# Layer 0's attention: the order of some VectorE operations, and the engine of a few others

## The chip, the cores and the metric

The kernel runs on one core of a Trainium2 chip. A core has five engines, each with a queue of its own that it works through in order: TensorE (PE: matmuls; PEld is its weight load), VectorE (DVE), ScalarE (ACT), GpSimd (POOL) and SyncE (SP, which here only issues transfers). Semaphores hold an engine until what it needs is there. The metric is device time in microseconds.

## The reference, cut to what matters

Two layers of a transformer trunk over 512 latent and 256 context tokens, width 1024. In each layer a modulated norm and one input projection give attention operands (`q`, `k`, `v`) and the two inputs of a gated mixer (`u`, `vg`); both results go through one output projection, then a feed-forward part follows.

```python
def chunk_gmlp(u, vg, w_s, b_s, g_norm):
    b, n, _ = u.shape
    u = jax.nn.gelu(u)
    vg = group_layernorm(jax.nn.gelu(vg).reshape(b, n, N_GMLP_GROUPS, GMLP_GROUP_DIM),
                         g_norm.reshape(N_GMLP_GROUPS, GMLP_GROUP_DIM))
    vc = vg.reshape(b, n // CHUNK, CHUNK, N_GMLP_GROUPS, GMLP_GROUP_DIM)
    mixed = jnp.einsum('gpq,bnqgc->bnpgc', w_s, vc) + b_s.T[None, None, :, :, None]
    return u * mixed.reshape(b, n, GMLP_DIM)

for l in range(DEPTH):
    ...
    attn_lat = gqa_blocks(qh_l, k_all, v_all)
    gm_lat = chunk_gmlp(u_l, g_l, w_spatial[l], b_spatial[l], gmlp_norm_g[l])
    x_lat = x_lat + ga1 * (jnp.concatenate([attn_lat, gm_lat], axis=-1) @ w_out[l])
    x_lat = x_lat + ga2 * sqrelu_mlp(modulate(rmsnorm(x_lat, norm2_g[l]), sh2, sc2),
                                     w_ff1[l], w_ff2[l])
```

Layer 0 does the same for the context tokens, whose queries see only the context's 256 keys.

## The kernel before

**Products.** Large products are taken from two parts of each operand, a rounded high one and the remainder, in three matmuls (high by high, high by low, low by high). `split` makes the parts: ACT casts the high one (L221), DVE or POOL subtracts to get the low one (L222). Weights go through a ring: SP loads `raw`, and `split` fills `hi` and `lo`. The low parts of the output projection's weights are made on POOL.

**The gated mixer of layer 0.** The 768 tokens are taken as three pairs of 128-token chunks and two halves of the channels: six *mixing halves*, numbered n = 0 to 5. The fifth half is n = 4, the last n = 5. For each, `sink_g` takes the projected bank through a GELU (L817 to L822) to `s`. Then `rest` computes mean and variance of four groups (L874, L875), adds an epsilon (L877), takes the inverse root on POOL (L298, by `rsqrt`), normalises the four groups in place (L880, four instructions) and splits `s` into `e` (ACT) and a low part (`acc` on DVE for the last half, a second `e` on POOL otherwise). `mixing` multiplies with the spatial weights `ws` into a PSUM bank `pt` (L217), scales and adds the bias on DVE (L905, two instructions, which empty the bank) and multiplies with `u` on POOL (L910, into `C`). When all are done, `make_gm` splits the gated result into the operands `A0` to `A3` of the output projection: a cast on ACT (L783) and a subtraction (L784), on POOL for the first two and on DVE for the other two.

**Attention of layer 0.** The context block (four pairs of query heads, two heads, two tiles) comes first. `attn_tile` makes the scores in a bank `pa`, their maximum on DVE (L999), the exponential on ACT (L1002, `w`), its reciprocal on DVE (L1004) and a copy of it on POOL (L1007). Later pieces transpose `w` on PE (L1018) into a `pt` bank, and split it with a cast on ACT (L1020) and a subtraction on DVE (L1021), then multiply with V (`third`, L1042 to L1045).

**What fills the gaps.** While attention runs, PE also works on the second half of layer 0's modulation (L354, its sums turned by L362 and L367 and added by L437), and then on the output projection of the gated result, whose results DVE adds into the residual (L954). The constants of the next layer are loaded and scaled by `consts`: the pack `k2` is issued by ACT (L652), then L660 twice, L671 and L674 scale it on DVE.

**What sets the order.** One program text is traced in order, and the engine queues follow from it. A planner, `Flow`, has a virtual time that matmuls move ahead. `defer(delay, f)` sets a due time for a piece, and `tick` runs what is due. `PAR` holds these delays: `G0` is 13600 from the end of `rest` to `mixing`; for the last half of layer 0, `rest` itself is deferred by 8000 and `mixing` by 8000 + `G0`. A scheduler then orders the instructions of each engine within that. DVE, ACT and POOL run what stands in their queues strictly in order.

## Time and profile before

| | us |
|---|---|
| median of 3 runs | 1482.96 (1482.33 to 1485.31) |
| the profiled execution | 1483.62 |
| its span | 1481.5 |
| mean granted PE clock | 0.998 |
| ACT busy | 635.9 (43%) |
| POOL busy | 363.5 (25%) |

The profile is of one execution; its time stands beside its span, and what lies around the span is 2.1 us. A row of the timeline gives start, duration, engine, line, operation and operands, then in brackets how long the engine sat idle before it and what ended that. Line numbers are those of the kernel before. In the 35 us from 165 to 200 us all of the instructions stand that the change moves.

### The profile page before, as it was taken

Reading aid. Unit: us, or ns where it says so; the run is one execution under the profiler, and the core shown is the slowest. Engines: PE = TensorE matmul, PEld = TensorE weight load, DVE = VectorE, ACT = ScalarE, POOL = GpSimd, SP = SyncE. Lnnn points to the kernel's source line nnn. Section 1 sums busy time; section 2 is a strip of 40 time slices with the busy share of each in tenths; the row PEclk is TensorE's granted clock in tenths of the full one; section 3 lists DMA queues with packets and bytes.
Section 4 is the critical chain, followed back from the end, with each engine's and each line's share of the span. In section 5 each row is a group of like instructions: output and inputs, shape, how many; then the busy total and the mean of one; then the engine's idle time right before and its main releaser. Section 6 shows DMA issues by size and latency. Waiting matters only on the chain.

```text
span 1481.5 us, 21923 instructions
## 1 busy us (share of the span) xinstructions
PE 1446.6 (98%) x8626; PEld 1275.9 (86%) x8626; DVE 879.6 (59%) x1543; ACT 635.9 (43%) x1081; POOL 363.5 (25%) x347
## 2 busy tenths in 40 slices
PE   6999899999999999999999999999999999999998
PEld 2899677898899999999989989998899888888887
DVE  5857767787755554544454437867877554444443
ACT  3552446673545453334334224536865322332221
POOL 0323521322064461413132213166122000000000
PEclk9999999999999999999999999999999999999999
DMA  9322444101233333424333311222001333222221
GB/s 367 111 72 83 167 148 160 58 16 58 75 121 121 115 121 107 142 100 135 107 128 114 100 43 58 101 72 61 26 1 59 128 100 99 89 97 100 100 100 57
DMA packets 50087, 148.78 MB, mean 100 GB/s; under 512 B 5440, under 2 KB 6976, under 8 KB 49984
## 3 DMA queue, kind: packets, MB, share of 16 engines
q1 hardware_dynamic: 49408, 146.72, 29.4%
q8 instruction: 68, 1.11, 0.3%
q10 hardware_dynamic: 576, 0.66, 0.1%
q14 instruction: 35, 0.29, 0.1%
HBM read 145.26 MB, written 2.10 MB: 99 GB/s over the span
## 4 chain that ended last, share of the span: by engine, by line
PE 85%; DVE 7%; ACT 3%; POOL 2%; issue 2%; DMA 1%; SPq 0%; POOLq 0%; ACTq 0%; DVEq 0%
PE pa L217 55%; PE pb L217 22%; PE pt L1018 3%; PE pt L217 2%; PE pb L354 2%; POOL m L298 1%; DVE s L880 1%; POOL lo L222 1%; DVE lo L222 1%; DMA A<-in_w_mod 1%; PE pt L735 1%; ACT hi L221 0%; DVE bn L874 0%; DVE s L822 0%; ACT w L1002 0%
## 5 line engine op out<-in xcount | busy, mean ns | idle before, releaser
L217 PE MATMUL pa<-A,hi 128*128 128x384 f32 (+2 forms) x1664 | 441.1, 347 | 1.0 <-DVE s L706 0.8
L221 ACT CAST hi<-raw 128x1024 fp32r<-128x1024 f32 x168 | 176.4, 1051 | 449.3 <-PE pa L217 364.6
L222 DVE TENSOR_TENSOR lo<-raw,hi 128x1024 fp32r<-128x1024 f32 x152 | 193.7, 1275 | 230.9 <-ACT hi L221 227.3
L217 PEld LDWEIGHTS pa<-A,hi 128*128 128x128 f32 x1664 | 299.4, 188 | 21.9 <-DVE s L706 1.0
L217 PE MATMUL pa<-A,lo 128*128 128x384 f32 (+2 forms) x832 | 287.9, 346 | 0.0
L217 PE MATMUL pa<-B,hi 128*128 128x512 f32 (+1 forms) x900 | 241.0, 355 | 0.0
L403 POOL TENSOR_TENSOR C<-C,s 128x512 f32<-128x512 f32 x112 | 162.9, 1469 | 310.7 <-ACT s L402 309.4
L217 PEld LDWEIGHTS pa<-B,hi 128*128 128x128 f32 x900 | 159.7, 189 | 24.2
L217 PEld LDWEIGHTS pa<-A,lo 128*128 128x128 f32 x832 | 156.5, 188 | 10.1
L217 PE MATMUL pa<-B,lo 128*128 128x512 f32 (+1 forms) x450 | 159.5, 355 | 0.0
L217 PE MATMUL pb<-B,hi 128*128 128x512 f32 (+1 forms) x600 | 157.3, 350 | 2.0 <-DVE X L954 2.0
L954 DVE SCALAR_TENSOR_TENSOR X<-pa,modT,X 128x512 f32<-128x512 f32 x126 | 79.4, 658 | 128.7 <-PE pa L217 128.7
L954 DVE SCALAR_TENSOR_TENSOR X<-pb,modT,X 128x512 f32<-128x512 f32 (+3 forms) x116 | 70.9, 619 | 82.2 <-PE pb L217 82.0
L217 PE MATMUL pb<-hi,A 128*128 128x256 f32 (+1 forms) x608 | 118.1, 291 | 0.6 <-DVE m L715 0.6
L217 PEld LDWEIGHTS pb<-B,hi 128*128 128x128 f32 x600 | 103.6, 189 | 16.5 <-DVE X L954 3.0
L217 PE MATMUL pb<-B,lo 128*128 128x512 f32 (+1 forms) x300 | 104.1, 347 | 0.0
L217 PEld LDWEIGHTS pb<-hi,A 128*128 128x128 f32 x608 | 97.0, 191 | 2.2 <-PE pb L217 0.8
L402 ACT ACTIVATE s<-k,silu 128x512 f32<-128x512 f32 x112 | 77.1, 716 | 44.8 <-DMA k<-in_w_mod 31.0
L217 PEld LDWEIGHTS pa<-B,lo 128*128 128x128 f32 x450 | 84.9, 189 | 12.0
L217 PE MATMUL pb<-lo,A 128*128 128x256 f32 (+1 forms) x304 | 87.7, 288 | 0.0
L217 PE MATMUL pb<-A,hi 128*128 128x384 f32 (+2 forms) x288 | 80.9, 361 | 2.3 <-ACT A L783 0.9
L1021 DVE TENSOR_TENSOR A<-pt,A 128x384 fp32r<-128x384 f32 (+1 forms) x144 | 73.1, 535 | 9.9 <-ACT A L1020 8.2
(197 smaller groups left out, 2221.8 us busy)
## 6 DMA issues: line engine op xcount, KB each, us to landing
raw<-in_w_ff SPq DMA_DIRECT2D x128, 512.0 KB, 3.5
k<-in_w_mod SPq DMA_DIRECT2D x96, 256.0 KB, 3.0
raw<-in_w_tok SPq DMA_DIRECT2D x16, 512.0 KB, 3.5
raw<-in_w_out SPq DMA_DIRECT2D x16, 512.0 KB, 3.5
lo<-in_w_mod SPq DMA_DIRECT2D x16, 512.0 KB, 4.5
hi<-in_w_mod SPq DMA_DIRECT2D x16, 512.0 KB, 4.0
A<-in_w_mod SPq DMA_DIRECT2D x8, 512.0 KB, 10.1
B<-in_w_mod SPq DMA_DIRECT2D x8, 512.0 KB, 9.5
```

Of the source, the lines that this page charges most:

```text
L217: pe.matmul(out, a, b, start=start, stop=stop)
L221: act.copy(hi, src)
L222: (eng or vec).tensor_tensor(out=lo, in0=src, in1=hi.bitcast(F32), op=ALU.subtract)
L298: pool_e.tensor_tensor(out=y, in0=v, in1=mhalf[:, 0:n], op=ALU.pow)
L354: pe.matmul(ps[q:q + 32, :], S32[:, k, :], ws_[k2 // 2][:, k2 % 2 * 512:(k2 % 2 + 1) * 512], start=k < ns, stop=k >= KT - ns)
L402: act.activation(p, w, AF.Copy, scale=s)
L403: pool_e.tensor_tensor(out=a, in0=a, in1=p, op=ALU.add)
L735: pe.transpose(p[:, o:o + 128], stk[:, t, hh, c0:c0 + 128].bitcast(F32), ident)
L880: (pool_e if l in PAR['VG'] else vec).tensor_scalar(v[:, i * 128:i * 128 + 128], v[:, i * 128:i * 128 + 128], mv[:, i, 0:1], r[:, i:i + 1] ...
L954: vec.scalar_tensor_tensor(out=xs, in0=src[:, s - off:e - off], scalar=modT[l][:, i * 8 + m, cond:cond + 1], in1=xs, op0=ALU.mult, op1=ALU ...
L1018: pe.transpose(tp_[:, (kt - k0) * 128:(kt - k0) * 128 + 128], p[:, kt * 128:kt * 128 + 128], ident)
L1021: vec.tensor_tensor(out=ptl[:, k0:k0 + step, d], in0=src, in1=pth[:, k0:k0 + step, d].bitcast(F32), op=ALU.subtract)
```

## The change

It has four parts, all in layer 0's attention.

- The last two mixing halves. `rest` is cut in two: `first` (statistics and inverse root) and `rest` (normalisation and split). The normalisation of the fifth half is issued behind the first attention tile's maximum (`maxes[0]`), that of the last half behind the second L905 of the half before (`evicted`). Four due times in `PAR` (`E0` to `E3`) take the place of the 8000 and of the sum with `G0`.
- All four low parts of `make_gm` are made on DVE, in layer 0 behind the fourth tile's maximum (`maxes[3]`) where there is one.
- The last of the six gated products (L910) is made on DVE.
- The next layer's constants are scaled on ACT.

```diff
@@ -39,7 +39,7 @@
        "FG0": [[0, 1], [2, 3]], "FG1": [[0, 1], [2], [3]], "QK0": 10000.0, "QK1": 9300.0, "TURN0": 3600.0,
        "TURN1": 5800.0, "G0": 13600.0, "G1": 22100.0, "T0": 6600.0, "T1": 7000.0, "TC": 1000.0, "PV0": 3100.0,
        "PV1": 9800.0, "NC": 21600.0, "REL": 4100.0, "MV": 260.0, "NP": 14, "P0": 1600.0, "P1": 3400.0, "PC": 1300.0,
-       "N001": 3500.0, "N010": 1800.0, "N011": 2000.0, "N101": 2600.0, "N110": 2000.0, "N111": 3900.0}
+       "N001": 3500.0, "N010": 1800.0, "N011": 2000.0, "N101": 2600.0, "N110": 2000.0, "N111": 3900.0, "E0": 9000.0, "E1": 8000.0, "E2": 11000.0, "E3": 20100.0}


 def once(fn):
@@ -657,7 +657,7 @@
         G = const.tile([128, 2, 2, 4, 64], F32, tag="G", name=nm("G"))
         for i, nme, s in ((0, "qg", HD ** -0.5), (1, "kg", 1.0)):
             g = P2(nme).rearrange("p (a b) -> p a b", a=2)
-            vec.tensor_scalar_mul(g, g, s)
+            (act.mul if l else vec.tensor_scalar_mul)(g, g, s)
             for hf in range(2):
                 gb = lambda a: g[:, a, :].unsqueeze(1).broadcast_to([128, 4, 32])
                 vec.tensor_tensor(out=G[:, i, 0, :, hf * 32:hf * 32 + 32], in0=cs[:, 0], in1=gb(hf), op=ALU.mult)
@@ -668,10 +668,10 @@
         ws = const.tile([128, 2, 512], F32R, tag="ws", name=nm("ws"))
         split(ws[:, 0, :], ws[:, 1, :], wr)
         if l:
-            vec.tensor_scalar_mul(P2("bs"), P2("bs"), 0.5)
+            act.mul(P2("bs"), P2("bs"), 0.5)
         gnh = const.tile([128, 4], F32, tag="gnh", name=nm("gnh"))
         g0 = PK1["gn"][0] + l * 4
-        vec.tensor_scalar_mul(gnh, c1[:, g0:g0 + 4], 0.5)
+        (act.mul if l else vec.tensor_scalar_mul)(gnh, c1[:, g0:g0 + 4], 0.5)
         return P2, G, ws, gnh

     def layer(l, h, nxt, K, kv=None, kv0=0):
@@ -781,7 +781,8 @@
                 gm = unit(f"A{g}", [128, 2, T])
                 src = U[g // 2][:, g % 2, 0:TQ]
                 act.copy(gm[:, 0, 0:TQ], src)
-                (pool_e if g < 2 and not last else vec).tensor_tensor(out=gm[:, 1, 0:TQ], in0=src, in1=gm[:, 0, 0:TQ].bitcast(F32), op=ALU.subtract)
+                with behind(maxes[3] if l == 0 and len(maxes) > 3 else None):
+                    vec.tensor_tensor(out=gm[:, 1, 0:TQ], in0=src, in1=gm[:, 0, 0:TQ].bitcast(F32), op=ALU.subtract)
                 GM.append(gm)

         def sink_q(grp):
@@ -859,7 +860,10 @@
                 else:
                     gelu2(u, src, [128, n])

-        mixes = []
+        mixes, maxes, evicted = [], [], {}
+
+        def behind(i):
+            return tc.issue_after(i.ins) if i is not None else nullcontext()

         def sink_g(gp):
             def f(tp, ps):
@@ -867,7 +871,7 @@
                 vg, n = [], len(mixes)

                 @once
-                def rest():
+                def stats():
                     st = small(24, tag="bn", bufs=2).rearrange("p (a b) -> p a b", b=6)
                     mv = small(8, tag="mv", bufs=2).rearrange("p (a b) -> p a b", b=2)
                     for i in range(4):
@@ -875,9 +879,22 @@
                         vec.bn_aggr(out=mv[:, i, :], in_=st[:, i, :])
                     ve = small(4)
                     vec.tensor_scalar(ve, mv[:, :, 1], 4 * EPS, None, op0=ALU.add)
-                    r = rsqrt(ve, 4, 1)
-                    for i in range(4):
-                        (pool_e if l in PAR['VG'] else vec).tensor_scalar(v[:, i * 128:i * 128 + 128], v[:, i * 128:i * 128 + 128], mv[:, i, 0:1], r[:, i:i + 1], op0=ALU.subtract, op1=ALU.mult)
+                    return mv, rsqrt(ve, 4, 1)
+
+                got = []
+
+                @once
+                def first():
+                    got.append(stats())
+
+                @once
+                def rest():
+                    first()
+                    mv, r = got[0]
+                    tail = l == 0 and n >= 2 * NP - 2
+                    with behind(maxes[0] if tail and n % 2 == 0 and maxes else evicted.get(n - 1) if tail and n % 2 else None):
+                        for i in range(4):
+                            (pool_e if l in PAR['VG'] else vec).tensor_scalar(v[:, i * 128:i * 128 + 128], v[:, i * 128:i * 128 + 128], mv[:, i, 0:1], r[:, i:i + 1], op0=ALU.subtract, op1=ALU.mult)
                     if n > 1:
                         mixes[n - 2]()
                     if l:
@@ -902,16 +919,21 @@
                     for g in range(2):
                         G_ = gp * 2 + g
                         to = u if G_ == LATE[l] else e
-                        vec.scalar_tensor_tensor(out=to[:, g, :].rearrange("p (t q) -> p t q", t=2), in0=mx[:, g, :].rearrange("p (t q) -> p t q", t=2),
+                        evicted[n] = vec.scalar_tensor_tensor(out=to[:, g, :].rearrange("p (t q) -> p t q", t=2), in0=mx[:, g, :].rearrange("p (t q) -> p t q", t=2),
                                                  scalar=gnh[:, G_:G_ + 1], in1=P2("bs")[:, G_ * 128:G_ * 128 + 128].unsqueeze(1).broadcast_to([128, 2, 128]),
                                                  op0=ALU.mult, op1=ALU.add)
                     gs = [g for g in range(2) if gp * 2 + g != LATE[l]]
                     gs = slice(gs[0], gs[-1] + 1)
-                    pool_e.tensor_tensor(out=u[:, gs], in0=e[:, gs], in1=u[:, gs], op=ALU.mult)
+                    (vec if l == 0 and n == 2 * NP - 1 else pool_e).tensor_tensor(out=u[:, gs], in0=e[:, gs], in1=u[:, gs], op=ALU.mult)
                 mixes.append(mixing)
                 if l == 0 and n == 2 * NP - 1:
-                    fl.defer(8000.0, rest)
-                    fl.defer(8000.0 + PAR["G0"], mixing)
+                    fl.defer(PAR["E1"], first)
+                    fl.defer(PAR["E2"], rest)
+                    fl.defer(PAR["E3"], mixing)
+                elif l == 0 and n == 2 * NP - 2:
+                    first()
+                    fl.defer(PAR["E0"], rest)
+                    fl.defer(PAR["G0"], mixing)
                 else:
                     rest()
                     fl.defer(PAR["G%d" % l], mixing)
@@ -996,7 +1018,7 @@
                 for i, kk in enumerate((kA, kB)):
                     mm(ps[:, o:o + n], Q[j][:, hh, qs], kk[:, kvh, koff + o:koff + o + n], i == 0, i == 1, n)
             nmx = small(1)
-            vec.tensor_reduce(out=nmx, in_=ps[:, 0:nk], axis=AX.X, op=ALU.max, negate=True)
+            maxes.append(vec.tensor_reduce(out=nmx, in_=ps[:, 0:nk], axis=AX.X, op=ALU.max, negate=True))
             p = tw([128, nk])
             sm = small(1)
             act.activation(p, ps[:, 0:nk], AF.Exp, bias=nmx, accum_out=sm)
```

`tc.issue_after(i)` tells the scheduler that what is issued in the block stands behind the instruction `i` of the same engine; it adds no semaphore.

The rows below are the engines' queues, in order: line, operation, output, inputs, shape and repeats. Line numbers of the changed kernel are higher: L999 is L1021 there, L1004 is L1026, L880 is L897, L818 and L822 are L819 and L823, L905 is L922, L784 is L785, L1021 is L1043, L1043 is L1065. First DVE around the first attention tile, before; `s_1713` is the fifth half, `s_1801` the last, `pa_1806` the tile's scores:

```order
L880 TENSOR_SCALAR s_1713<-s_1713,mv_1719,m_1730 128x128 x4
L999 TENSOR_REDUCE m_1809<-pa_1806 128x1
L818 SCALAR_TENSOR_TENSOR s_1801<-s_1801,pb_1740 128x512
L1004 RECIPROCAL m_1814<-m_1812 128x1
L822 SCALAR_TENSOR_TENSOR s_1801<-s_1801,pb_1740 128x512
```

And now, where the last half is `s_1793` and the scores are `pa_1798`:

```order
L1021 TENSOR_REDUCE m_1801<-pa_1798 128x1
L819 SCALAR_TENSOR_TENSOR s_1793<-s_1793,pb_1732 128x512
L1026 RECIPROCAL m_1806<-m_1804 128x1
L897 TENSOR_SCALAR s_1713<-s_1713,mv_1719,m_1730 128x128 x3
L823 SCALAR_TENSOR_TENSOR s_1793<-s_1793,pb_1732 128x512
L897 TENSOR_SCALAR s_1713<-s_1713,mv_1719,m_1730 128x128
```

The maximum stands ahead of the four normalisations, and with it the reciprocal and a GELU step. On POOL the two L784 that stood behind the fifth half's inverse root are gone; the fifth half's low `e`, which stood behind them, now stands behind the first tile's copy.

The second place is DVE at the fifth half's L905 and the last half's normalisation, before:

```order
L877 TENSOR_SCALAR m_1981<-mv_1972 128x4
L999 TENSOR_REDUCE m_2006<-pa_2003 128x1
L880 TENSOR_SCALAR s_1801<-s_1801,mv_1972,m_1983 128x128 x4
L1004 RECIPROCAL m_2011<-m_2009 128x1
L222 TENSOR_TENSOR acc_350_1990<-s_1801,e_1989 128x512
L905 SCALAR_TENSOR_TENSOR s_1953<-pt_1940,gnh_173,k_5_96 128x256 x2
L1021 TENSOR_TENSOR A_331_1917<-pt_1957,A_330_1916 128x2x128
```

And now:

```order
L785 TENSOR_TENSOR A_386_2101<-C_100_482,A_386_2101 128x768
L1026 RECIPROCAL m_1931<-m_1929 128x1
L881 TENSOR_SCALAR m_1981<-mv_1972 128x4
L785 TENSOR_TENSOR A_387_2104<-C_100_482,A_387_2104 128x768
L1021 TENSOR_REDUCE m_1998<-pa_1995 128x1
L922 SCALAR_TENSOR_TENSOR s_1953<-pt_1940,gnh_173,k_5_96 128x256 x2
L1043 TENSOR_TENSOR A_331_1917<-pt_1957,A_330_1916 128x2x128
L1065 TENSOR_TENSOR mix_1962<-pb_1963,pv_1968 64x256
L1026 RECIPROCAL m_2003<-m_2001 128x1
L1021 TENSOR_REDUCE m_2028<-pa_2025 128x1
L437 TENSOR_TENSOR modT_90<-pt_1989,c_70 128x8
L897 TENSOR_SCALAR s_1793<-s_1793,mv_1972,m_1983 128x128 x4
```

The two subtractions of `make_gm` have come in, L905 stands ahead of the last half's normalisation, and that half's low part `acc` follows four rows further on. POOL's order here is L910 of the fifth half, a copy L1007, then the subtraction of a weight split (L222, `lo`), as before. On ACT the cast of the last half to `e` now stands behind that weight's cast (L221, `hi`), before it stood ahead of it.

The third place is ACT at the next layer's constants (`k_964` is the pack, `gnh` its gains), before:

```order
L652 DMA k_964_4567<-in_pk 128x640
L783 CAST A_388_2107<-C_101_483 128x768
L783 CAST A_389_2110<-C_101_483 128x768
L1020 CAST A_392_2133<-pt_2135 128x2x128
L1042 COPY pv_2146<-pb_2141 64x256
L1002 ACTIVATE w_2154,m_2155<-pa_2149,m_2152 128x256
```

And now:

```order
L652 DMA k_964_4567<-in_pk 128x640
L783 CAST A_388_2107<-C_101_483 128x768
L783 CAST A_389_2110<-C_101_483 128x768
L1042 CAST A_392_2133<-pt_2135 128x2x128
L1042 CAST A_392_2133<-pt_2175 128x2x128
L1024 ACTIVATE w_2185,m_2186<-pa_2180,m_2183 128x256
L660 ACTIVATE k_964_4567<-k_964_4567 128x64 x2
L671 ACTIVATE k_964_4567<-k_964_4567 128x512
L674 ACTIVATE gnh_4588<-c_70 128x4
L399 ACTIVATE C_973_4620<-k_4618,silu 128x512
L1042 CAST A_412_2206<-pt_2208 128x2x128
```

Four instructions came from DVE, and they stand ahead of the modulation's L399 and the next cast. On DVE the last gated product stands behind L437, where L674 was. SP's queue is the same in both kernels, and outside this stretch no engine's order differs.

## The prediction

> **What bounds the kernel now.** I read the share of each engine first, then windows over the stretch that the change touches and over what follows it, then PE's waits in that stretch.
>
> ```profile
> PE 1446.6 (98%) x8626; PEld 1275.9 (86%) x8626; DVE 879.6 (59%) x1543; ACT 635.9 (43%) x1081; POOL 363.5 (25%) x347
> ...
> 165.00:200.00 35.00, 28.43 (x190) 17.52 (x190) 26.80 (x73) 17.68 (x44) 20.20 (x21) 0.95 0.58 211
> 200.00:240.00 40.00, 40.00 (x267) 33.43 (x266) 26.33 (x67) 18.42 (x48) 4.99 (x15) 1.00 0.45 159
> 240.00:1481.50 1241.50, 1229.81 (x7184) 1097.49 (x7183) 715.53 (x1135) 530.74 (x865) 296.18 (x268) 1.00 0.27 89
> ```
>
> TensorE (PE) is busy 98% of the span, so only what keeps PE waiting, or its clock low, can be won. In the windows the columns are length, busy time of PE, weight loads, DVE, ACT and POOL, then granted clock and DMA share. From 165 to 200 us, where all moved instructions lie, PE works 28.43 of 35.00 us: 6.57 us idle. Right behind it PE is never idle (40.00 of 40.00) and later nearly never, in an order that the change leaves as it was. What is won or lost here therefore reaches the end undiminished.
>
> ```profile
> PE pt L1018 <- ACT w L1002: 4.1, 2, 3.9
> PE pb L217 <- ACT A L783: 0.9, 1, 0.9
> PE pt L367 <- DVE s L905: 0.8, 1, 0.8
> PE pb L217 <- DVE A L784: 0.6, 1, 0.6
> ```
>
> PE's waits of that stretch (total, times, longest) come to 4.1 + 0.9 + 0.8 + 0.6 = 6.4 us, which is the idle time. The largest, 3.9 us, is the transpose L1018 of the first context attention tile, which wants the exponential L1002. The rows around it, DVE and POOL first:
>
> ```profile
> 159.15 1.11 DVE L880 TENSOR_SCALAR s<-s,mv,m 128x128 f32<-128x128 f32 x4 [1.12 <-POOL m L298]
> ...
> 166.10 4.11 DVE L880 TENSOR_SCALAR s<-s,mv,m 128x128 f32<-128x128 f32 x4 [1.12 <-POOL m L298]
> 170.13 0.41 DVE L999 TENSOR_REDUCE m<-pa 128x1 f32<-128x256 f32 x1
> ...
> 166.03 3.58 POOL L784 TENSOR_TENSOR A<-C,A 128x768 fp32r<-128x768 f32 x2
> ...
> 171.26 0.47 ACT L1002 ACTIVATE w<-pa,m 128x256 f32<-128x256 f32 x1
> ...
> 171.87 0.69 PE L1018 MATMUL pt<-c,w 128*128 128x128 f32 x2 [3.92 <-ACT w L1002]
> ```
>
> The four normalisations L880 of the fifth mixing half take 4.11 us here, and 1.11 us one half earlier. The difference, 3.0 us, lies beside two subtractions L784 on POOL (166.03 to 169.61). The maximum L999 starts 170.13, right behind the last L880, then the exponential, then PE at 171.87. So VectorE's order, not data, holds the first tile.
>
> ```profile
> 168.00:171.00 3.00, 0.00 (x0) 0.00 (x0) 2.54 (x4) 0.76 (x2) 1.68 (x2) 1.00 0.85 295
> 171.00:174.00 3.00, 2.13 (x12) 1.03 (x12) 1.95 (x7) 1.70 (x5) 1.45 (x2) 0.59 0.98 399
> 174.00:177.00 3.00, 3.00 (x16) 0.74 (x12) 2.99 (x13) 1.87 (x4) 1.44 (x2) 0.84 0.07 27
> ```
>
> A second price follows in the clock column: (1 − 0.59) × 3 + (1 − 0.84) × 3 = 1.71 us of clock lost behind the idle stretch. At half clock that is 3.42 us. The last row's 0.48 puts its end at 174.96, so its start at 171.54; 0.33 us of it passed before PE worked at all (171.87). Lost work: 1.71 − 0.17 = 1.54 us.
>
> **The change part by part.** The first two edits are one. L880 of the fifth half goes behind the maximum, and the first two L784 leave POOL for VectorE, far later. This removes the 3.92 us. The 1.54 us go with it: 0 to 1.54, and I take all, as no lower clock shows beside the shorter waits (0.95 mean clock over 35 us is 1.75 us, and 1.71 of it is this one). [...]
>
> The later waits, and what stands around them:
>
> ```profile
> 181.05 1.56 PE L217 MATMUL pt<-ws,e 128*128 128x128 f32 x12
> 186.42 0.25 PE L367 MATMUL pt<-s,c 128*32 128x8 f32 x8 [0.82 <-DVE s L905]
> 189.22 0.42 PE L217 MATMUL pt<-ws,e 128*128 128x128 f32 x2
> 194.13 0.44 PE L217 MATMUL pb<-A,hi 128*128 128x384 f32 x1 [0.92 <-ACT A L783]
> 195.13 0.44 PE L217 MATMUL pb<-A,hi 128*128 128x384 f32 x1 [0.55 <-DVE A L784]
> 196.13 0.33 PE L1018 MATMUL pt<-c,w 128*128 128x128 f32 x1 [0.21 <-ACT w L1002]
> ...
> 184.15 0.62 ACT L221 CAST e<-s 128x512 fp32r<-128x512 f32 x1 [1.49 <-DVE s L880]
> ...
> 184.80 0.69 DVE L222 TENSOR_TENSOR acc<-s,e 128x512 fp32r<-128x512 f32 x1 [0.61 <-ACT e L221]
> 185.41 0.87 DVE L905 SCALAR_TENSOR_TENSOR s<-pt,gnh,k 128x256 f32<-128x256 f32 x2
> ```
>
> With the 3.92 these are 0.82 + 0.92 + 0.55 + 0.21 = 2.50 us. The 0.82 us exist because L905, which frees a PSUM bank, stands on DVE behind `acc` of the last half, and that behind ACT's cast. In the new order L905 comes first, right behind its matmuls: the wait goes. What is late next is the last half itself, whose normalisation now stands behind L905.
>
> ```profile
> 186.93 0.41 DVE L999 TENSOR_REDUCE m<-pa 128x1 f32<-128x256 f32 x1
> ...
> 187.59 2.38 POOL L222 TENSOR_TENSOR lo<-raw,hi 128x1024 fp32r<-128x1024 f32 x1
> ```
>
> Count from the end of the fifth half's matmuls (181.05 + 1.56 = 182.61). PE asks for the last half's `e` at 189.22, 6.61 us later, or 5.8 without the 0.82 wait. DVE's pieces from L905 to this maximum took 185.41 to 187.34 = 1.93 us; nearly the same now stand ahead of L880, so DVE reaches it after about 2.0. Undisturbed, `e` is there after 2.0 + 1.11 + 0.62 = 3.7: 2.1 us to spare. But POOL starts its weight split (2.38 us) after L905 and one gated product, 0.87 + 1.3 = 2.2: within 0.3 us of L880. Whichever L880 meets it is held. At worst 2.38 more makes 6.1, 0.3 late, and ACT now has a weight cast of about a microsecond (1051 ns below) ahead of `e`: 1.3 late, and the rest of `acc` 0.2 or so behind. I take 1.5 us, by the 166.10 row, where L880 beside POOL did wait; the ends are 0 and 2.38.
>
> ```profile
> 191.93 1.29 POOL L910 TENSOR_TENSOR C<-s,C 128x512 f32<-128x512 f32 x1
> ...
> 192.00 1.24 DVE L674 TENSOR_SCALAR gnh<-c 128x4 f32<-128x4 f32 x1
> 194.11 1.83 DVE L784 TENSOR_TENSOR A<-C,A 128x768 fp32r<-128x768 f32 x2 [0.55 <-ACT A L783]
> ...
> 193.25 1.57 ACT L783 CAST A<-C 128x768 fp32r<-128x768 f32 x2 [2.09 <-DVE gnh L674]
> ```
>
> The last gated product L910 took 1.29 us on POOL, and ACT's L783 started when it ended (193.22). VectorE did not run it here; its bounds are 0.69 (`acc`, same size, two inputs) and 1.29 (POOL itself). I take 0.69, as no POOL work stands beside it. It starts where L674 started and ends some 0.6 to 0.7 us before POOL did. So of the 0.92 about 0.2 remain, the 0.55 remain (L784 still follows L783), and the 0.21 go: 0.75 us in all, between 0 and 1.47.
>
> The two L784 added to DVE cost 1.83 us of it, and L910 0.69; L674 (1.24) and the rows below (0.29, 0.42) go, as do the 3.0 us held at 166.10. DVE thus does 2.4 us less in a stretch where it has 8 us idle. POOL does 3.58 + 1.29 less.
>
> ```profile
> 198.10 0.29 DVE L660 TENSOR_SCALAR k<-k 128x64 f32<-128x64 f32 x2
> 198.31 0.42 DVE L671 TENSOR_SCALAR k<-k 128x512 f32<-128x512 f32 x1
> ...
> 195.97 0.72 ACT L399 ACTIVATE C<-k,silu 128x512 f32<-128x512 f32 x1
> ...
> k<-in_pk ACTq DMA_DIRECT2D x1, 320.0 KB, 3.4
> ...
> A<-in_w_mod SPq DMA_DIRECT2D x8, 512.0 KB, 10.1
> ...
> L221 ACT CAST hi<-raw 128x1024 fp32r<-128x1024 f32 x168 | 176.4, 1051 | 449.3 <-PE pa L217 364.6
> ```
>
> The constants on ACT: four instructions, from 0.88 us (DVE's durations, with 0.17 for L674) to 4 × 0.72 = 2.9; I take 1.5, near the wide one at 0.72 and three small ones. ACT has 17 of 35 us idle, so I cost them at nothing. Behind them queue two L399 and the casts that empty transposes; if that cover fails they cost up to 1.5. The first of them waits for the constants' DMA, which lands 3.4 us after its issue. By the order, an issue (some 0.3), both L783 (1.57), two casts and an exponential stand between, some 3 us: a wait of 0.4, at nothing too. SP's order is unchanged, so no transfer moves.
>
> Sum: −3.92 − 1.54 − 2.50 + 1.5 + 0.75 = −5.71 us. The profiled execution took 1483.62 us (span 1481.5); −5.7 gives 1477.9. The median of the runs, 1482.96, is 0.66 lower: **1477.3 us**.
>
> **The rivals.** All are put on the median.
>
> *L880 of the last half passes ahead of POOL's split.* For it: the two starts are 0.3 us apart. Against: one held L880 of four is enough. Without the 1.5 us: −7.2, 1475.8.
>
> *VectorE's new subtractions are held by POOL.*
>
> ```profile
> L222 DVE TENSOR_TENSOR lo<-raw,hi x152: 1192/1224/2364, 47.3 to 1450.9; 128x1024 fp32r<-128x1024 f32 x152
> ...
> L222 POOL TENSOR_TENSOR lo<-raw,hi x16: 2354/2390/2848, 176.8 to 1032.8; 128x1024 fp32r<-128x1024 f32 x16
> ```
>
> DVE's splits, which like L784 read two SBUF operands, take 1.22 us in the middle and up to 2.36. POOL's splits (2.39) begin at 176.8, just where the first two L784 now stand on DVE, ahead of a maximum and a reciprocal. Such a hold moves that tile's exponential by up to 2.39; if it is not covered, PE waits about 2.2 more: −3.5, 1479.5. Against it: later tiles are queued on PE. [...]
>
> *The change does not do what it says.* The first wait stays because the exponential is late for another reason (ACT's activation ahead of it, or the scores), with its clock loss: only 2.50 − 2.25 is won, 1482.7. Against it: L999 started 0.02 us behind L880's end (170.21), while PE had been idle for over 2 us.
>
> *ACT is parked by the constants' DMA, and it is slower.* If that transfer took not its 3.4 us but the 10.1 of the large weight loads, ACT, 3 us behind the issue, would stand 7.1 us with the transposes' casts behind it. PE would wait for them and lose a clock window again: −5.71 + 7.1 + 1.54 = +2.9, 1485.9, or somewhat more. From a landing of about 7.2 us (3 + 5.71 − 1.54) the gain is gone. Against it: its own row, 3.4, and a DMA share of 0.58 in this stretch.
>
> **How the numbers follow.** Forecast 0.48; L880 passes 0.20; subtractions held 0.20; no effect 0.07; ACT parked 0.05. The range takes the first three. Below, the 1475.8 with 1.0 us for the 0.75 and small parts, 1474.8; above, the 1479.5 with 0.7 us for the constants' uncovered part, 1480.2. What it leaves out is the last two cases and a little at both ends. About 0.2%, 3 us, is what a measurement of this kernel can tell from no change: under 1480.0 counts as faster. A quarter of the third case crosses that: faster 0.48 + 0.20 + 0.15 = 0.83, same 0.07 + 0.05 = 0.12, slower 0.05.
>
> **What the profile afterwards would show.** Right: no PE wait above 2.4 us between 160 and 200, clock 1.00 there, L880 of the fifth half near 1.1 us in all, the wait at L367 gone, and one at the last half's mixing matmuls. Rival one shows that last wait missing; rival two, an L784 of over 1.5 us with a transpose waiting behind it; rival four, ACT idle for the constants' transfer. The prediction is wrong if the first wait is still there, or if PE's busy share falls after 200.

## The result, and the profile after

| | before | changed |
|---|---|---|
| median of 6 runs each, us | 1482.64 | 1477.37 |
| lowest to highest, us | 1481.12 to 1485.31 | 1474.87 to 1478.26 |
| ratio (95% interval) | | 0.9958 (0.9947 to 0.9968) |
| profiled execution, us | 1483.62 | 1474.87 |
| its span, us | 1481.5 | 1473.1 |

The change makes the kernel 5.3 us faster by the medians, 6.2 by the ratio. The two profiled executions differ by more, 8.4 us of span. To see where, I cut the span at two instructions that are the same in both kernels: the first L880 of the fourth mixing half and the fourth of the additions L437 (226.59 us before). What lies between is called *the stretch*; it is given by the row of the windows view that holds exactly this piece. The columns are as in the prediction: length, busy PE, weight loads, DVE, ACT, POOL, granted clock, DMA share, GB/s. Before:

```profile
159.15:226.59 67.44, 60.87 (x409) 46.16 (x408) 46.83 (x130) 31.91 (x80) 24.84 (x32) 0.97 0.48 171
```

And changed:

```profile
156.82:218.06 61.24, 59.82 (x409) 46.00 (x408) 45.16 (x128) 32.92 (x84) 22.02 (x29) 1.00 0.54 188
```

Both hold 409 matmuls. The stretch is 6.20 us shorter: PE's idle time fell from 67.44 − 60.87 = 6.57 to 1.42 us, and its busy time by 1.05 us, with the clock at 1.00 instead of 0.97. Behind the stretch the two kernels take the same time (1481.5 − 226.6 = 1254.9, and 1473.1 − 218.1 = 1255.0). The remaining 2.33 us were won ahead of it (159.15 against 156.82), where the change touches nothing. There the clock differed in these two executions; before, then changed, the window from 20 to 40 us:

```profile
20.00:40.00 20.00, 19.11 (x108) 10.76 (x112) 14.44 (x24) 8.43 (x14) 1.02 (x2) 0.91 1.04 398
```

```profile
20.00:40.00 20.00, 19.23 (x116) 10.54 (x115) 14.14 (x22) 9.53 (x17) 1.58 (x3) 1.00 1.04 397
```

So one profiled execution against another tells the change only by the stretch. Its start moved between 156.4 and 159.4 us over all fourteen profiles, whatever the kernel. In these two, the clock of before is 0.50 from 21.35 to 24.76 us, and the changed kernel's is 1.00 all the way to the stretch. Of the other twelve, eight hold 1.00 in the stretch and 0.997 to 0.999 over the span, so they lost clock outside it.

PE's waits in the stretch, changed (they answer to the four of before):

```profile
PE pt L1040 <- DVE modT L437: 0.6, 1, 0.6
PE pt L217 <- DVE acc L222: 0.5, 1, 0.5
PE pb L354 <- DVE s L362: 0.2, 1, 0.2
```

None of the old four is left. The first attention tile, changed, on DVE, ACT and PE:

```profile
163.17 0.43 DVE L1021 TENSOR_REDUCE m<-pa 128x1 f32<-128x256 f32 x1 [0.52 <-PE pa L217]
...
164.31 0.84 DVE L897 TENSOR_SCALAR s<-s,mv,m 128x128 f32<-128x128 f32 x3
...
163.63 0.47 ACT L1024 ACTIVATE w<-pa,m 128x256 f32<-128x256 f32 x1
...
165.45 0.40 PE L1040 MATMUL pt<-c,w 128*128 128x128 f32 x2
```

The maximum (now L1021) runs as soon as PE has the scores, the exponential 0.03 us after it, and the transposes come without a wait. The normalisations (now L897) stand behind and take 0.84 for three: nothing holds them.

The last half, changed: its normalisation, then its low part `acc` on DVE, its weight neighbours on ACT and POOL, and PE.

```profile
173.14 1.75 DVE L785 TENSOR_TENSOR A<-C,A 128x768 fp32r<-128x768 f32 x1
...
174.95 0.95 DVE L785 TENSOR_TENSOR A<-C,A 128x768 fp32r<-128x768 f32 x1
...
178.38 1.10 DVE L897 TENSOR_SCALAR s<-s,mv,m 128x128 f32<-128x128 f32 x4
...
181.01 1.40 DVE L222 TENSOR_TENSOR acc<-s,e 128x512 fp32r<-128x512 f32 x1
...
178.35 1.05 ACT L221 CAST hi<-raw 128x1024 fp32r<-128x1024 f32 x1 [0.81 <-PE pt L1040]
...
171.72 2.36 POOL L222 TENSOR_TENSOR lo<-raw,hi 128x1024 fp32r<-128x1024 f32 x1
...
174.02 1.97 POOL L1029 COPY rc<-m 128x64 f32<-128x64 f32 x2
...
179.48 2.38 POOL L222 TENSOR_TENSOR lo<-raw,hi 128x1024 fp32r<-128x1024 f32 x1 [0.94 <-ACT hi L221]
...
182.47 0.33 PE L217 MATMUL pt<-ws,acc 128*128 128x128 f32 x1 [0.53 <-DVE acc L222]
186.09 0.63 PE L1040 MATMUL pt<-c,w 128*128 128x128 f32 x4 [0.63 <-DVE modT L437]
```

L897 ends (179.48) in the very moment in which POOL's split starts, and is not held. What is held is `acc`, four rows on: 1.40 us instead of 0.69 (184.80 before), while the three rows between took 0.42, 0.16 and 0.72 us beside the same split. PE waits 0.53 for it. The first L785 was held in the same way beside POOL's split of 171.72 (1.75 us; the second took 0.95), and nobody waited for it. Beside both, POOL's two copies L1029 took 1.97 us, to 175.99, where the second L785 had just ended (175.90); two such copies took 0.41 us in the kernel before (181.59).

The row names PE as what released ACT's cast at 178.35, but that cast reads only a loaded weight, and the record of this load gives the time: issued at 172.20, landed 6.1 us later, at 178.3. In the execution below the same load was issued at 171.83 and landed after 5.2 us, at 177.0, and the cast began at 177.09. So POOL's split waits here for the weight.

### The profile page after: what moved, and what is told of

Its sections match the earlier page's. It is cut to its first block, busy times and chain, and to the rows that moved or that the text cites. A ratio compares the mean times of both kernels' runs of the same rounds, so it can differ in the third digit from the quotient of the medians.

```text
span 1473.1 us, 21926 instructions
## 1 busy us (share of the span) xinstructions
PE 1443.7 (98%) x8626; PEld 1275.3 (87%) x8626; DVE 875.6 (59%) x1542; ACT 637.2 (43%) x1085; POOL 362.5 (25%) x344
## 4 chain that ended last, share of the span: by engine, by line
PE 87%; DVE 6%; ACT 2%; POOL 2%; issue 1%; DMA 1%; SPq 0%; POOLq 0%; ACTq 0%; DVEq 0%
PE pa L217 55%; PE pb L217 23%; PE pt L1040 3%; PE pt L217 2%; PE pb L354 2%; POOL m L298 1%; PE pt L735 1%; DVE lo L222 1%; DMA A<-in_w_mod 1%; POOL lo L222 1%; ACT hi L221 0%; DVE s L897 0%; ACT w L1024 0%; DVE s L706 0%; DVE X L976 0%
## 5 line engine op out<-in xcount | busy, mean ns | idle before, releaser
L221 ACT CAST hi<-raw 128x1024 fp32r<-128x1024 f32 x168 | 176.4, 1051 | 446.4 <-PE pa L217 363.4
L222 DVE TENSOR_TENSOR lo<-raw,hi 128x1024 fp32r<-128x1024 f32 x152 | 191.8, 1262 | 231.1 <-ACT hi L221 227.5
L1043 DVE TENSOR_TENSOR A<-pt,A 128x384 fp32r<-128x384 f32 (+1 forms) x144 | 73.1, 536 | 10.2 <-ACT A L1042 8.7
```

Of the source, the lines that this page charges most:

```text
L221: act.copy(hi, src)
L222: (eng or vec).tensor_tensor(out=lo, in0=src, in1=hi.bitcast(F32), op=ALU.subtract)
L1043: vec.tensor_tensor(out=ptl[:, k0:k0 + step, d], in0=src, in1=pth[:, k0:k0 + step, d].bitcast(F32), op=ALU.subtract)
```

## The experiments

All start from the changed kernel unless said otherwise. Each is judged by its stretch; what is not said to be timed has one profile.

**The changed kernel again.** No edit.

> The changed kernel once more, for how far one profile repeats. Measure: the stretch from the first L880 of the fourth mixing half to the last modulation addition L437 at 226.59 us of before; 67.43 us before, 61.24 us after. My theory: the stretch repeats within 0.3 us (60.9 to 61.6), and whatever the whole time differs from the 1474.87 of the first profile is spent before that stretch, in the first 60 us. Rival: the stretch itself differs by over 1 us from run to run, and one profile proves little.

```profile
156.43:218.36 61.93, 59.58 (x409) 45.96 (x408) 46.28 (x129) 32.92 (x84) 21.61 (x29) 1.00 0.54 186
```

```profile
178.02 3.17 DVE L897 TENSOR_SCALAR s<-s,mv,m 128x128 f32<-128x128 f32 x4
...
178.21 2.37 POOL L222 TENSOR_TENSOR lo<-raw,hi 128x1024 fp32r<-128x1024 f32 x1
```

61.93, 0.3 above what I gave it, and the 0.7 us that this span is longer (1473.8 against 1473.1) lie in the stretch, not ahead of it. Here POOL's split starts 0.19 us after the first L897, and the four take 3.17 us; PE waits 1.48 us at the last half's matmuls, where the first profile has 0.53 us. These are two outcomes of one program, by when a weight arrives.

**The first two L784 on POOL again**, with the order kept:

```diff
-                with behind(maxes[3] if l == 0 and len(maxes) > 3 else None):
-                    vec.tensor_tensor(out=gm[:, 1, 0:TQ], ...
+                with behind(maxes[3] if l == 0 and g > 1 and len(maxes) > 3 else None):
+                    (pool_e if g < 2 and not last else vec).tensor_tensor(out=gm[:, 1, 0:TQ], ...
```

> As changed, but the first two L784 on POOL again (the order of the maximum ahead of L880 stays). Stretch 61.24 us as changed. My theory: POOL's two L784 hold whatever L880 comes beside them, some 3.0 us, also when the maximum stands ahead; L905, L1021 and the transposes behind them come 2 to 3 us late, so PE waits 1.5 to 3 us at the second tiles' transposes, without a lower clock: stretch 62.7 to 64.2. Rival: the order alone is the cure, since the held L880 have time: 61.2 to 61.7.

```profile
158.02:220.97 62.95, 59.53 (x409) 45.84 (x408) 46.01 (x126) 32.83 (x84) 24.16 (x31) 1.00 0.52 183
```

```profile
165.52 3.34 DVE L897 TENSOR_SCALAR s<-s,mv,m 128x128 f32<-128x128 f32 x3
...
164.91 3.61 POOL L785 TENSOR_TENSOR A<-C,A 128x768 fp32r<-128x768 f32 x2
```

As my theory had it. Three L897 take 3.34 us instead of 0.84: they end one normalisation behind POOL's pair (165.52 + 3.34 = 168.86; 164.91 + 3.61 = 168.52, and 0.34 for one more). What stands behind is late and PE waits 0.82 and 1.28 us one tile on. Against the 61.24 to 62.11 of three profiles as changed, keeping L784 on POOL costs 0.8 to 1.7 us. The last half's wait is 0.43 us here, close to the 0.53 of the first of those profiles, so 1.7 is the closer figure. The order by itself, with the smaller parts, thus brings 67.44 − 62.95 = 4.5 us.

**The fifth half ahead of the first maximum again**, L784 on VectorE, twice:

```diff
-                    with behind(maxes[0] if tail and n % 2 == 0 and maxes else evicted.get(n - 1) if tail and n % 2 else None):
+                    with behind(evicted.get(n - 1) if tail and n % 2 else None):
...
-                elif l == 0 and n == 2 * NP - 2:
-                    first()
-                    fl.defer(PAR["E0"], rest)
-                    fl.defer(PAR["G0"], mixing)
```

> As changed, but the fifth half's L880 ahead of the first maximum again; L784 stay on VectorE. My theory: without POOL's L784 beside them the four L880 take 1.1 us instead of 4.1, the maximum starts 1.1 to 1.7 us later than as changed (163.17), and PE waits about 0.5 us for the first exponential, at full clock: stretch 61.5 to 62.2. Rival: the place behind L880 itself is what cost; the wait of nearly 4 us and the half clock return: 65.5 to 66.5.

> The kernel with the fifth half's L880 ahead of the first maximum once more. My theory: its waits of 0.93 and 0.99 us at the first two tiles' transposes belong to it and return, the half clock of 6.83 us behind the wait of 1.65 us was one run's window: stretch 62.8 to 63.8 (61.24 or 61.93 as changed, plus the 1.9 us of waits). Rival: the clock is part of it, 65.5 to 66.5 again.

```profile
156.70:222.72 66.02, 62.29 (x409) 48.90 (x408) 46.94 (x128) 32.88 (x84) 21.63 (x29) 0.95 0.50 175
...
182.35:185.76 3.41, 1.76 (x13) 1.39 (x11) 3.38 (x8) 1.36 (x3) 1.09 (x2) 1.00 0.95 322
185.76:189.17 3.41, 3.41 (x22) 2.95 (x21) 2.67 (x10) 1.52 (x5) 0.97 (x2) 0.50 0.35 135
189.17:192.59 3.42, 3.42 (x16) 3.42 (x16) 2.49 (x6) 2.36 (x5) 0.24 (x1) 0.50 0.33 94
```

Its waits:

```profile
PE pt L1036 <- ACT w L1020: 1.9, 2, 1.0
PE pt L217 <- ACT e L221: 1.7, 1, 1.7
```

The second profile:

```profile
156.97:222.85 65.88, 62.26 (x409) 48.84 (x408) 46.77 (x128) 32.80 (x84) 21.58 (x29) 0.95 0.50 176
```

The numbers fell where the rival had put them, but not for its reason, so the row that decides is not the length. The nearly 4 us wait did not come back: the four L897 took 1.12 us, and the first tile's wait is 0.93 us, with 0.99 at the next. What came back is the half clock, in another place: for 6.8 us behind the wait of 1.65 us at the last half's matmuls (1.5 in the second profile). PE's busy time is 62.3 instead of 59.6 to 59.8 (the two profiles as changed), so the clock costs 2.5 to 2.7 us. My second expectation, that this was one run's window, is wrong too: it came in both profiles (0.95 in both rows). Without the clock the order of the fifth half is worth the two waits, 1.9 us. Whether the half clock belongs to this order or only to the wait at the last half's matmuls stays open: as changed that wait of about 1.5 us comes too, once without a half clock (above) and once with one (below).

**The last half in its old place**, ahead of the fifth half's L905:

```diff
-                    with behind(maxes[0] if tail and n % 2 == 0 and maxes else evicted.get(n - 1) if tail and n % 2 else None):
+                    with behind(maxes[0] if tail and n % 2 == 0 and maxes else None):
...
-                    fl.defer(PAR["E1"], first)
-                    fl.defer(PAR["E2"], rest)
-                    fl.defer(PAR["E3"], mixing)
+                    fl.defer(8000.0, rest)
+                    fl.defer(8000.0 + PAR["G0"], mixing)
```

> As changed, but the last half's normalisation in its old place (ahead of the fifth half's L905). My theory: the wait of 0.82 us at L367 behind L905 returns, and the 0.53 us wait for the last half's low part (which took 1.40 instead of 0.69 beside POOL's weight split) goes: stretch 61.3 to 61.8. Rival: the last half's place is worth nothing or was a loss: 60.5 to 61.2.

```profile
157.91:219.30 61.39, 59.30 (x409) 45.66 (x408) 44.57 (x129) 32.74 (x84) 21.87 (x29) 1.00 0.54 188
```

and its largest wait:

```profile
PE pt L367 <- DVE s L922: 1.3, 1, 1.3
```

61.39 is within the expectation. The wait at L367 is back and has grown (1.27 us), the wait at the last half's matmuls is gone. As changed it is 61.24 to 62.11: this part of the change exchanges one wait for another and is worth nothing that these profiles can show.

**The last gated product on POOL again**:

```diff
-                    (vec if l == 0 and n == 2 * NP - 1 else pool_e).tensor_tensor(out=u[:, gs], ...
+                    pool_e.tensor_tensor(out=u[:, gs], ...
```

> As changed, but the last gated product on POOL again. Stretch as changed: 61.24 and 61.93 us in two profiles, without any wait at the gated operands A2 and A3. POOL takes 1.29 instead of 0.69 us, so L783 and L784 come 0.6 us later. My theory: they had 0.3 to 0.4 us to spare, so PE waits 0.2 to 0.6 us at a matmul on them, and nothing else moves: 61.5 to 62.5. Rival: the product's engine is worth nothing, other work covers it: no such wait.

```profile
157.51:220.06 62.55, 59.81 (x409) 45.93 (x408) 45.60 (x128) 33.01 (x84) 22.84 (x30) 1.00 0.52 184
```

and its wait at a gated operand:

```profile
PE pb L217 <- DVE A L785: 0.4, 1, 0.4
```

In this profile the last half's wait is 1.47 us, so it compares with the 61.93 of the repeat: 0.6 us more. Of this 0.4 us are idle time of PE, the expected wait at L785; the other 0.2 are busy time (59.81 against 59.58), which differs by as much between the two profiles as changed.

**The next layer's constants on VectorE again**:

```diff
-            (act.mul if l else vec.tensor_scalar_mul)(g, g, s)
+            vec.tensor_scalar_mul(g, g, s)
...
-            act.mul(P2("bs"), P2("bs"), 0.5)
+            vec.tensor_scalar_mul(P2("bs"), P2("bs"), 0.5)
...
-        (act.mul if l else vec.tensor_scalar_mul)(gnh, c1[:, g0:g0 + 4], 0.5)
+        vec.tensor_scalar_mul(gnh, c1[:, g0:g0 + 4], 0.5)
```

> As changed, but the next layer's constants on VectorE again. L674 stands ahead of L784 and, with no gated product on POOL beside it, takes 0.17 us and not 1.24. My theory: the move to ACT is worth at most 0.2 us: no wait at L783 or L784 above 0.2, stretch 61.2 to 62.1. Rival: ACT's move was needed, a wait of 0.5 us or more at L783 or L784 returns.

```profile
159.36:220.48 61.12, 59.70 (x409) 46.03 (x408) 45.76 (x132) 32.17 (x80) 22.02 (x29) 1.00 0.54 188
```

and L674 in its timeline:

```profile
189.76 0.15 DVE L674 TENSOR_SCALAR gnh<-c 128x4 f32<-128x4 f32 x1
```

No wait at L783 or L784, 61.12: moving the constants is worth nothing here. L674 took 1.24 us before, where POOL's gated product ran beside it (191.93 to 193.22), and 0.15 us here, where POOL has no such work.

**The kernel before, with the first two L784 on VectorE and no order told**:

```diff
-                (pool_e if g < 2 and not last else vec).tensor_tensor(out=gm[:, 1, 0:TQ], ...
+                vec.tensor_tensor(out=gm[:, 1, 0:TQ], ...
```

> The kernel before, with the first two L784 on VectorE and nothing else: without an order told they stand between the fifth half's L880 and the first maximum. My theory: L880 then take 1.1 us and the two L784 1.8, 2.9 us in all instead of 4.1 held ones, so the first wait falls by 1.2 us only, to about 2.7, and the low clock behind it stays, since in one run a wait of 1.65 us within a 3.4 us window was enough for it: stretch 65.9 to 66.6, nearly that of before (67.43). Rival: without the hold the clock stays high, 64.5 to 65.2. Second rival: freeing POOL is the whole cure: under 63.5.

```profile
157.66:222.87 65.21, 59.54 (x409) 45.70 (x408) 45.89 (x132) 32.02 (x80) 22.14 (x30) 1.00 0.50 178
```

and DVE at the first tile:

```profile
164.62 1.12 DVE L880 TENSOR_SCALAR s<-s,mv,m 128x128 f32<-128x128 f32 x4 [1.12 <-POOL m L298]
165.66 1.82 DVE L784 TENSOR_TENSOR A<-C,A 128x768 fp32r<-128x768 f32 x2
167.39 0.42 DVE L999 TENSOR_REDUCE m<-pa 128x1 f32<-128x256 f32 x1
```

and its first two waits:

```profile
PE pt L1018 <- ACT w L1002: 2.9, 3, 2.0
PE pt L367 <- DVE s L905: 1.1, 1, 1.1
```

The order is as I had it, 2.9 us ahead of the maximum, but my theory missed: the first wait is 1.99 us, not 2.7, and the clock stays at 1.00. The length is that of the first rival, at its upper end. Of the 6.2 us this one line brings 2.2: 1.93 of the first wait and 1.33 of busy time (60.87 − 59.54), less what grew elsewhere (0.72 at the next tile, 1.14 for 0.82 at L367). The rest needs the order.

**The third output weight's split behind the last half's cast**, so that POOL's subtraction starts late; that weight is used later, and PE waits for it nowhere in the stretch. In `pump` the split is put aside, and in `rest` of the last half it is issued behind ACT's cast:

```diff
+            if held is None and key == ("out", 0, 0, 2) and not state.get("half"):
+                behind_half.append((hi, lo, raw, pool_e))
...
+                    cast = split(*vg, v, pool_e if l in PAR['VL'] and n < 2 * NP - 1 else vec)
+                    if l == 0 and n == 2 * NP - 1:
+                        state["half"] = 1
+                        while behind_half:
+                            with tc.issue_after(cast.ins):
+                                split(*behind_half.pop(0))
```

> As changed, and the third output weight's cast on ACT is put behind the last half's cast to e, so that POOL's subtraction of 2.4 us for it starts when the last half's normalisation and most of its low part are done. That weight is used some 20 us later. My theory: the wait at the last half's mixing matmuls (0.53 us in one profile, 1.48 in the other, as the weight arrived later or earlier) falls to 0.3 or less, the 0.63 us at the transpose stays: stretch 60.4 to 60.9, whenever the weight arrives. Rival: the weight's cast holds up ACT's next exponential instead, and the wait at the transpose grows as much: 61.2 to 61.9.

> The kernel with the third output weight's split behind the last half's cast once more, timed beside the changed kernel. First profile 60.62 us of stretch, with 0.74 us at the last half's matmuls (now behind ACT's order) and none at the transpose. My theory: its stretch repeats within 0.3 us, whenever the weight lands, and the time is 0.5 to 1.3 us below the changed kernel's, which the start of the program (up to 2.5 us from run to run) may hide. Rival: it varies as the changed kernel's does.

```profile
159.26:219.88 60.62, 59.35 (x409) 45.94 (x408) 44.69 (x129) 32.90 (x84) 22.02 (x29) 1.00 0.55 190
```

and its waits:

```profile
PE pt L217 <- ACT e L221: 0.7, 1, 0.7
PE pb L217 <- DVE mix L1075: 0.3, 1, 0.3
```

The second profile:

```profile
158.13:219.03 60.90, 59.59 (x409) 46.01 (x408) 44.51 (x128) 33.04 (x84) 21.99 (x29) 1.00 0.55 191
```

60.62 and 60.90, with the same two waits in both. Neither wait is as expected: 0.74 us remain at the last half's matmuls, since ACT's cast to `e` now stands behind a copy and a cast that wait for PE, and the one at the transpose went instead. The order on DVE differs too: two operations stand between the first L897 and the other three, and `acc` comes later, so the late split is not the only thing that changed.

Timed side by side, this kernel takes 1475.93 us (median of 5, 1474.58 to 1476.68; ratio to before 0.9945, 0.9932 to 0.9957), the changed kernel 1478.37 (next), and before 1484.09. It is the fastest of the three. Against the changed kernel the two intervals overlap, and the medians, 2.4 us apart, hold different granted clocks. At the same clock, 0.997, two of its runs took 1476.44 and 1476.68 us, and four of the changed kernel 1477.53 to 1478.95, so 0.9 to 2.5 us are its own; the stretch shows 0.3 to 1.5 us.

**The changed kernel a third time**, timed beside it:

> The changed kernel, timed beside the one above, and a third profile. My theory: either 61.2 to 61.4 (the weight is late, the low part of the last half is held: 0.5 us of wait) or 61.8 to 62.0 (the weight is early, an L880 is held: 1.5 us), nothing between; about 5.5 us below the kernel before in time. Rival: other values, and the arrival of the weight is not what decides.

```profile
158.29:220.40 62.11, 60.45 (x409) 47.20 (x408) 46.36 (x129) 33.03 (x84) 21.61 (x29) 0.97 0.52 186
...
182.72:186.13 3.41, 2.36 (x17) 2.19 (x18) 3.35 (x10) 1.56 (x4) 0.24 (x1) 1.00 0.94 357
186.13:189.54 3.41, 3.41 (x22) 2.95 (x21) 2.72 (x10) 2.28 (x7) 1.10 (x3) 0.50 0.14 41
```

1478.37 us (1476.64 to 1478.95), ratio to before 0.9961 (0.9947 to 0.9974). 62.11 is a third value, which I had excluded. The weight lands early, as in the second profile (issued at 173.68, 5.2 us), and the L897 are held (1.51 us of wait); what is new is that the clock halves for 3.4 us behind that wait. The 0.63 us wait at the transpose doesn't appear beside it, and busy time is 0.6 to 0.9 us more (60.45 against 59.82 and 59.58).

**ACT's copies of attention's results (L1042) behind the cast too**, on top of the late split:

```diff
-                        state["half"] = 1
+                        state["half"] = cast
...
-                act.copy(t, o[64:128, 0:256])
+                with behind(state.get("half") if l == 0 else None):
+                    act.copy(t, o[64:128, 0:256])
```

> The kernel with the late split, with ACT's copies of the attention results (L1042) behind the last half's cast too, so that the cast waits for less. My theory: the 0.74 us wait at the last half's matmuls falls to 0.3 to 0.5, stretch 60.2 to 60.5. Rival: the copies now hold up the attention result and a wait of as much opens behind them: 60.6 or more.

```profile
157.76:218.79 61.03, 59.41 (x409) 45.95 (x408) 44.54 (x128) 32.88 (x84) 21.48 (x29) 1.00 0.54 189
```

The rival had it: the 0.74 us stay (the cast waits for another cast, not for the copy), and the 0.63 us at the transpose return. 61.03, no gain.

## Why the prediction held, point by point

The forecast for the stretch was −5.71 us. Three profiles of the changed kernel give 61.24, 61.93 and 62.11 against 67.44 in the one profile of before: −6.20, −5.51, −5.33.

- **The first wait (−3.92): held.** It is gone in each profile. The runs split its cause: with L784 on POOL and the order told, three L897 are held 3.34 us but the first tile is not, and 4.5 us are won, smaller parts included; with L784 on VectorE and no order, 1.99 us of wait stay, and 2.2 are won. The order is the larger half.
- **The clock behind it (−1.54): the size was off.** Busy time of PE fell by 1.05 us against the first profile and 1.29 against the second, so the half clock (0.50 from 171.53 to 174.95 us before, 3.42 us) cost two thirds to five sixths of what (1 − clock) × time gave.
- **The four later waits (−2.50): held**, all gone.
- **The last half (+1.5, from 0 to 2.38): held as a choice, and it is a choice in each run.** The prediction saw DVE and POOL within 0.3 us of each other. The runs show both: 1.48 and 1.51 us of wait where POOL's split starts within the four L897 (0.19 and 0.23 us behind the first one's start), 0.53 where it starts at their end (1.10 us). What decides, the landing of a weight, was in no term. I had not seen either that even then the low part `acc` is held (1.40 us): the rival of no wait at all did not occur.
- **The gated product (+0.75 left): wrong place, near size.** No wait is left at L783 or L784. It is 0.4 to 0.6 us more with POOL, by one profile. Instead 0.63 us appeared at a transpose that wants a PSUM bank, which L437 empties; L437 stands behind a reciprocal that waits for ACT (0.69 us), a maximum and two L922. That wait was in no term.
- **The constants on ACT (nothing): held.** They take 0.41 + 0.64 + 0.21 us there, ACT did not wait for their transfer in the changed kernel's first profile, and VectorE could have kept them.
- **VectorE's subtractions held by POOL (a rival): the hold happened, the wait did not.** The first L785 takes 1.75 us, the second 0.95, and PE has other work. Beside a POOL split stood the 1.75 us and, for `acc`, 1.40; where no such split ran, the same two operations took 0.95 and 0.69 us or less.
- **Clock 1.00 in this place: two of three.** The prediction charged no lost clock to the waits that stay, since none showed beside the short waits of before. The third profile as changed has a half clock behind a wait of 1.51 us, and the two with the fifth half in its old place have one behind 1.65 and 1.5 us. The other two profiles as changed hold 1.00.

Two readings were slightly off. L999 started 0.08 us ahead of the end of the last L880 (170.13 against 170.21), not 0.02 behind it, which changes nothing. The gated product's head start is 0.53 us by its own rows (193.22 less 192.00 + 0.69), not 0.6 to 0.7, which would have added 0.1 to 0.2 us to the sum.

That the median came out within 0.1 us of the forecast is luck. The errors cancel: the clock brought 0.25 to 0.5 us less than forecast and the 0.63 us at the transpose were not foreseen, but the 0.75 us for the gated product did not come and, in the first profile, the last half cost 0.53 instead of 1.5. Besides, the medians themselves move by more: 1477.37 and 1478.37 us for the changed kernel timed twice, 1482.64 and 1484.09 for the one before.

## What to carry to other kernels

When a short operation waits behind held ones in an in-order queue, ask first what its successor needs and put that ahead; taking the holder away alone brought a third of the gain, the order (with the smaller parts) about three quarters. Two engines that arrive at nearly the same time are a fork, not a cost: give both ends, ask what decides between them (here the landing of a weight, 5.2 or 6.1 us), and if the work of one of them is not urgent, order it away, which brought 0.3 to 1.5 us of the stretch here. Compare single profiles by a stretch between two instructions that both kernels have, since the start of this program alone moves by up to 3 us.

## What the runs showed of the hardware

The granted clock fell to 0.50 behind windows in which PE was idle, and behind others in which it was partly busy. In the profile of before it is 0.50 from 21.35 to 24.76 us and from 171.53 to 174.95; the two starts lie 150.18 us apart, 44 times 3.413, which is within 0.01 the length of each. With the fifth half in its old place it is 0.50 from 185.76 to 192.59 (first profile), in the third profile as changed from 186.13 to 189.54. In the 3.4 us ahead PE was busy 1.62 and 0.00 us in the profile of before, 1.76 in that of the fifth half and 2.36 in the third as changed. With 1.68 us busy, in the run with only L784 moved, and with 1.93 us, in the second profile as changed, no half clock followed:

```profile
166.73:170.14 3.41, 1.68 (x13) 0.71 (x13) 2.84 (x7) 1.61 (x5) 2.11 (x2) 1.00 1.00 366
...
178.81:182.22 3.41, 1.93 (x15) 1.69 (x14) 3.41 (x7) 1.17 (x4) 2.01 (x2) 1.00 0.73 227
```

So PE's busy time in such a window doesn't tell the two cases apart here, and what decides stays open. The half clock lasted 3.4 or 6.8 us, which cost about 0.6 to 1.3 and 2.5 to 2.7 us of PE's busy time here, and that can be more than the wait that it follows.

The spread of the timed runs goes with the granted clock, which is on record for each. Eleven timed runs of the changed kernel took 1474.87 us at 1.000, 1476.64 and 1476.93 at 0.999, 1477.34 to 1477.97 at 0.998 and 1477.53 to 1478.95 at 0.997; nine of the kernel before, timed side by side, went from 1481.39 at 0.998 to 1485.60 and 1485.62 at 0.994. That is about 1 us of time for each 0.001 of the clock, which is 1.5 us of lost clock. It also bears on the gain: at 0.997 the two kernels, timed side by side, lie 3.9 to 5.3 us apart (1482.84 against 1477.53 to 1478.95), less than their medians do (5.7), since the kernel before had the lower clock more often (median 0.996 against 0.997). Where in the program the timed runs lost their clock no trace shows.
